# Activation tiles moved onto multiples of 256 bytes from the weight tiles, and one set of embedding weights split one channel group earlier

## The chip, the cores and the metric

The kernel runs on one core of a Trainium2 chip. TensorE (PE in the profile; PEld is its loading of the stationary operand) multiplies from SBUF into PSUM, ScalarE (ACT) and VectorE (DVE) work on SBUF and PSUM, GpSimd (POOL) does a few small things, and SyncE (SP) issues the DMAs. The metric is the device time of one execution in microseconds; the kernel before took 1401.75 (median of 3 runs, 1401.49 to 1403.82).

## The reference

A trunk of four layers over 256 tokens of width 1024, in float32. Each layer adds to the residual stream h a mixer of its normalised input (latent attention in layers 0 and 3, a Conformer convolution in layer 1, a gated recurrence in layer 2), then a SwiGLU feed-forward of width 2816, then a per-layer embedding gated by h:

```
for i in range(DEPTH):
    h = h + mixer(_rmsnorm(h, norm1_g[i]))
    h = h + _swiglu(_rmsnorm(h, norm2_g[i]), ffn_w_gu[i], ffn_w_down[i])
    gate = sigmoid(_rmsnorm(h, ple_norm_g[i]) @ ple_w_gate[i])
    h = h + (p[i] @ ple_w_proj[i]) * gate
```

The convolution of layer 1 is a gated pointwise product (2048 columns, one half through a sigmoid), a causal depthwise filter of 31 taps over each of 1024 channels, a layer norm over the channels, a swish and a second pointwise product (w_pw2).

## The kernel before

**Products.** A float32 weight tile arrives by DMA in a tile `raw`, and is split into two tiles in the matmul's rounded float32 format: ACT writes the high part `whi` (L189, or L194 where a norm's gain is multiplied in), DVE writes the rest `wlo` = raw - whi (L190 or L195). Activations are split in the same way after a transpose on TensorE (L259, L246, L247): `xT` for a whole normalised stream, `aT` for the gated inner values of the feed-forward, `cT` for attention's compressed vectors, `pT` for the embedding input. A product is three matmuls, high x high, low weights x high, high weights x low (`mm`, all recorded on L216). In most products the activation is stationary and 512 columns of weights move; in the convolution and in half of the recurrence the weights are stationary and 256 columns of xT move. In the profile's names `mm<-whi,xT` the tile behind the arrow is the one that moves, then the stationary one; `mm` and `acc` are PSUM banks.

**Where tiles lie.** Pools take SBUF one behind the other: constants, weights (`wpool`: 9 whi, 8 wlo, 4 raw tiles of 4096 bytes per partition), then `act` with everything that lives through the layers, then one pool per stage. Within a pool a tile stands behind those that were first asked for. Some of the tiles of `act` are scalars per token of 4 or 8 bytes, each of which takes 32; they stand between the large ones. The program's addresses, modulo 256:

| tiles | before | after |
|---|---|---|
| whi, wlo, raw, h | 224 | 224 |
| xT | 96 | 224 |
| pT, pph | 96 | 224 |
| th, hg, gain | 160 | 224 |
| aT, cT, and the stages' other first tiles | 160 | 224 |
| ident (constant) | 128 | 128 |

**The order of work.** Python issues the program; a scheduler places each instruction on its engine's queue, and each queue runs in that order. `self.fence` holds instructions behind which the next split of weights is to be issued (`behind`, around the splits in `granule` and `embed_weights`). In the convolution TensorE is pinned to the order in which the code is written.

**The convolution stage** (layer 1). For each of eight groups of 128 channels, c = 0 to 7, TensorE forms the pointwise product into a bank; ACT takes the sigmoid (L832) and DVE the gated value `glu` (L836): these two are `gate`. For c from 2 on the filter runs on TensorE: four DMAs per group make a shifted copy `win` (L763), one loads the taps as small matrices `tapw` (L767), 64 small matmuls sum them (`taps_pe`), and DVE (L782) or ACT turns the sum into `co`, of which ACT takes the square `sq` (L787). `moments` adds co and sq of two groups to the statistics on TensorE (`tr<-co,mean`, `tr<-sq,mean`). When all are in, `sums` is copied (L869), transposed by `tok`, copied (`st`, L874), and a chain of small DVE instructions gives scale and shift (dg, L884), which TensorE broadcasts (L885, `tr<-work,ones`). From there z, its swish and its split `yT` follow per group, and the product with w_pw2 (`linear_rows`, one weight granule per 128 rows). `embed_weights(2)` loads and splits p_t and two granules of ple_w_proj of the next layer; `embed(2)` multiplies them while the scale is worked out. Rows 0 to 4 of w_pw2 are split before the statistics, rows 5 to 7 during the swish.

Of the kernel before, what the change touches and what calls it, by code (L numbers as in the profile page):

```python
# [12 lines left out]
F32 = mybir.dt.float32  # L13
# [8 lines left out]
P = 128  # L22
# [29 lines left out]
GAINS = {}  # L52
for _k in GSIZE:
    GAINS[_k] = sum(GSIZE[j] * GCOUNT[j] for j in GAINS)


class Norm:
# [3 lines left out]
    def __init__(self, T, full=False, defer=False):  # L61
        self.T, self.full, self.defer = T, full, defer
        self.x, self.r = None, [None] * NT
# [64 lines left out]
class Trunk:  # L128
    def __init__(self, ctx, tc, a, out):
        self.ctx, self.tc, self.nc, self.a, self.out = ctx, tc, tc.nc, a, out  # L130
        nc = self.nc
        pool = lambda name, **k: ctx.enter_context(tc.tile_pool(name=name, **k))
        self.const = pool("const", bufs=1)
        self.wpool = pool("wpool", bufs=1)
        self.act = pool("act", bufs=1)
        self.ps = pool("ps", bufs=1, space=PSUM)
        self.n = 0
        self.fence = []
        self.head = None
        self.pinned = False  # L140
        self.pT, self.pph = {}, {}
        self.ident = self.const.tile([P, P], F32, name="ident")
        make_identity(nc, self.ident)
        self.gT = self.const.tile([P, a["gains"].shape[1]], F32, name="gT")
        self.h = [self.act.tile([P, D], F32, name=f"h{t}", tag=f"h{t}") for t in range(NT)]

    def nm(self, s):
# [8 lines left out]
        return self.bank("acc", 4)  # L156

    def tmp(self, tag, shape, bufs, dtype=F32, pool=None):
        return (pool or self.act).tile(shape, dtype, name=self.nm(tag), tag=tag, bufs=bufs)

    def scope(self, name):
        return self.tc.tile_pool(name=name, bufs=1)
# [404 lines left out]
    def mla(self, i, norm, done, pre):  # L567
# [8 lines left out]
        with self.scope(self.nm("mla")) as pool:  # L576
# [5 lines left out]
            for t in range(NT):  # L582
                xs, r = self.cut(norm.x, t), norm.r[t]
                pa, pb = self.acc(), self.acc()
                self.mms(pa[:, :QL], xs, [(hi[:, 0, :QL], lo[:, 0, :QL]) for hi, lo in gr])
                self.mms(pb[:, : KVL + ROPE], xs, [(hi[:, 0, QL : NC + ROPE], lo[:, 0, QL : NC + ROPE]) for hi, lo in gr])
                cg = tmp("cg", [P, NC], 1)
                nc.scalar.activation(cg[:, :QL], pa[:, :QL], AF.Copy)
                V.tensor_copy(cg[:, QL:], pb[:, :KVL])
                ss = tmp("css", [P, 2], 2)  # L590
                for c, (ps, n) in enumerate([(pa, QL), (pb, KVL)]):
                    nc.scalar.activation(self.tmp("junk", [P, 512], 1, BF16)[:, :n], ps[:, :n], AF.Square, scale=r, accum_out=ss[:, c : c + 1])
                kr = tmp("kr", [P, 1, ROPE], 2)
                nc.scalar.activation(kr[:, 0], pb[:, KVL : KVL + ROPE], AF.Copy, scale=r)
                self.split_T(cg, cT, 0, t)
                css.append(ss)
                krot.append(kr)
# [137 lines left out]
    def conv(self, i, norm, done, pre):  # L735
# [6 lines left out]
        PAD = TAPS - 1  # L742
# [3 lines left out]
        with self.scope(self.nm("conv")) as pool:  # L746
# [10 lines left out]
            def spread(c):  # L757

                win[c] = tmp("win", [P, QUAD, WIN], 3)
                for j in range(QUAD):  # L760
                    src = xin[c][32 * j : 32 * j + 32]
                    shifts = bass.AP(tensor=src.tensor, offset=src.offset, ap=[src.ap[0], [1, QUAD], [1, WIN]])
                    nc.sync.dma_start(win[c][:, j], shifts)  # L763

            def tap_weights(c):
                tapw[c] = tmp("tapw", [P, QUAD, STEPS, 32], 3)
                nc.sync.dma_start(tapw[c], a["conv_taps"][:, c])  # L767

            def taps_pe(c):
                ps = self.bank("mm", 2)[:, :S]  # L770
                for m in range(STEPS):
                    for j in range(QUAD):
                        self.matmul(
                            ps[32 * j : 32 * j + 32], tapw[c][:, j, m], win[c][:, j, QUAD * m : QUAD * m + S],
                            start=m == 0, stop=m == STEPS - 1,
                        )
                if c + 3 < KD:
                    tap_weights(c + 3)
                if c in BASE:
                    nc.scalar.activation(co[:, c], ps, AF.Identity, bias=par(c, TAPS))  # L780
                else:
                    V.scalar_tensor_tensor(out=co[:, c], in0=ps, scalar=par(c, TAPS), in1=self.base, op0=ALU.add, op1=ALU.subtract)  # L782
                    square(c)

            def square(c):
                sq[c] = tmp("sq", [P, S], 4)
                self.sq = nc.scalar.activation(sq[c], co[:, c], AF.Square)  # L787
# [15 lines left out]
            def chain(c, k0, k1):  # L803
                for k in range(k0, k1):
                    if k == 0:
                        V.tensor_scalar(out=co[:, c], in0=xin[c][:, :S], scalar1=par(c, 0), scalar2=par(c, TAPS), op0=ALU.mult, op1=ALU.add)
                    else:
                        V.scalar_tensor_tensor(out=co[:, c], in0=xin[c][:, k : k + S], scalar=par(c, k), in1=co[:, c], op0=ALU.mult, op1=ALU.add)

            def set_base():  # L810

                pm = self.bank("tr", 2)[:, :S]
                for b in BASE:
                    self.matmul(pm, self.mean, co[:, b], start=b == BASE[0], stop=b == BASE[-1])
                self.base = tmp("base", [P, S], 1)
                V.tensor_scalar(out=self.base, in0=pm, scalar1=KD / len(BASE), scalar2=None, op0=ALU.mult)
                for c in BASE:
                    V.tensor_tensor(out=co[:, c], in0=co[:, c], in1=self.base, op=ALU.subtract)
                    square(c)
# [4 lines left out]
            for c in range(KD):  # L824
                if c % 2 == 0:
                    ws = self.conv_head(i, c) if c else self.head
                ps = self.acc()
                for half in range(2):
                    s = slice(half * 256 + c % 2 * P, half * 256 + (c % 2 + 1) * P)
                    self.mms(ps[:, half * S : (half + 1) * S], [(hi[:, s], lo[:, s]) for hi, lo in ws], xs)  # L830
                sg = tmp("work", [P, S], 3)
                gate = [nc.scalar.activation(sg, ps[:, S:], AF.Sigmoid, bias=self.cb1[:, KD + c : KD + c + 1]).ins]  # L832
                x = xin[c] = tmp("glu", [P, PAD + S + 2], 4)
                nc.gpsimd.memset(x[:, :PAD], 0.0)
                nc.gpsimd.memset(x[:, PAD + S :], 0.0)
                glu = V.scalar_tensor_tensor(out=x[:, PAD : PAD + S], in0=ps[:, :S], scalar=self.cb1[:, c : c + 1], in1=sg, op0=ALU.add, op1=ALU.mult)  # L836
                gate.append(glu.ins)
                if c not in CHAINS:
                    spread(c)
                if c == 4:  # L840
                    taps_pe(2)
                if c == 5:
                    taps_pe(3)
                if c == 6:
                    set_base()
                    taps_pe(4)
                if c >= 2:
                    k = min(TAPS, 6 * (c - 1))
                    for b in CHAINS:
                        chain(b, 6 * (c - 2), k)  # L850
            taps_pe(5)
            moments(BASE)
            self.fence = gate
            self.embed_weights(2)
            rows = lambda k: self.granule([(a["conv_w_pw2"][0][k * P : (k + 1) * P], 0)], 1, D)
            ws = [rows(k) for k in range(5)]
            taps_pe(6)
# [319 lines left out]
```

## Time and profile before

| | |
|---|---|
| median of 3 runs | 1401.75 us |
| the profiled execution | 1402.8 us |
| its span, first to last instruction | 1401.0 us |
| mean granted TensorE clock | 0.992 |
| PE, DVE, ACT busy | 1352.4, 919.4, 789.7 us |

Matmuls are pipelined: the mean of one (about 400 ns for 512 columns) includes the way through the array and overlaps with the next, so the rate is read from start to start, or from pieces of the chain of waits, which give the time and the number of matmuls. That chain is followed back from the last instruction, at each step to what released it.

### The profile page before, as it was taken

Reading aid. Unit: us, or ns where it says so; the run is one execution under the profiler, and the core shown is the slowest. Engines: PE = TensorE matmul, PEld = TensorE weight load, DVE = VectorE, ACT = ScalarE, POOL = GpSimd, SP = SyncE. Lnnn points to the kernel's source line nnn. Section 1 sums busy time; section 2 is a strip of 40 time slices with the busy share of each in tenths; the row PEclk is TensorE's granted clock in tenths of the full one; section 3 lists DMA queues with packets and bytes.
Section 4 is the critical chain, followed back from the end, with each engine's and each line's share of the span. In section 5 each row is a group of like instructions: output and inputs, shape, how many; then the busy total and the mean of one; then the engine's idle time right before and its main releaser. Section 6 shows DMA issues by size and latency. Waiting matters only on the chain.

```text
span 1401.0 us, 20409 instructions
## 1 busy us (share of the span) xinstructions
PE 1352.4 (97%) x7153; PEld 1096.6 (78%) x7153; DVE 919.4 (66%) x1995; ACT 789.7 (56%) x1494; POOL 19.1 (1%) x52
## 2 busy tenths in 40 slices
PE   7899999999898999999999999999999999999997
PEld 6767878887875788887788887878878767888885
DVE  6867555558876855556887768555567776655556
ACT  6776555546525654555675546555556776555543
POOL 0100000000000000000000000000000000000000
PEclk9999999999998999999999999999999999999999
DMA  7524656536564655554474425555553433665532
GB/s 234 176 67 128 201 175 191 188 123 220 182 181 153 196 181 180 181 180 163 122 211 132 133 91 175 185 181 181 180 169 110 139 121 108 217 189 187 188 119 74
DMA packets 174023, 228.15 MB, mean 163 GB/s; under 512 B 11712, under 2 KB 138848, under 8 KB 173920
## 3 DMA queue, kind: packets, MB, share of 16 engines
q1 hardware_dynamic: 173920, 226.85, 51.6%
q8 instruction: 56, 0.92, 0.3%
q14 instruction: 47, 0.39, 0.1%
HBM read 222.27 MB, written 1.05 MB: 159 GB/s over the span
## 4 chain that ended last, share of the span: by engine, by line
PE 77%; DVE 8%; DMA 6%; ACT 6%; issue 2%; SPq 0%; DVEq 0%; ACTq 0%
PE mm L216 42%; PE acc L216 26%; PE tr L259 3%; DVE wlo L195 3%; ACT whi L194 2%; DMA raw<-in_ple_w_gate_dram 1%; PE acc L1020 1%; DMA raw<-in_conv_w_pw_dram 1%; DMA raw<-in_mla_w_in_dram 1%; DMA raw<-in_ffn_w_down_dram 1%; PE acc L659 1%; ACT p L669 1%; PE tr L641 1%; DVE wlo L190 1%; ACT whi L189 1%
## 5 line engine op out<-in xcount | busy, mean ns | idle before, releaser
L216 PE MATMUL mm<-whi,xT 128*128 128x512 f32 x1632 | 553.4, 402 | 1.0 <-ACT xT L246 0.7
L194 ACT ACTIVATE whi<-raw,gT 128x512 fp32r<-128x512 f32 (+3 forms) x604 | 387.7, 700 | 136.4 <-PE acc L216 60.1
L195 DVE SCALAR_TENSOR_TENSOR wlo<-raw,gT,whi 128x512 fp32r<-128x512 f32 (+3 forms) x604 | 410.4, 729 | 60.3 <-PE acc L216 33.9
L216 PEld LDWEIGHTS mm<-whi,xT 128*128 128x128 f32 x1632 | 306.3, 189 | 67.1 <-ACT xT L246 1.2
L216 PE MATMUL mm<-wlo,xT 128*128 128x512 f32 x816 | 323.7, 397 | 1.1 <-DVE wlo L190 1.1
L216 PE MATMUL acc<-whi,aT 128*128 128x512 f32 x704 | 234.5, 394 | 1.6 <-DVE aT L247 1.6
L190 DVE TENSOR_TENSOR wlo<-raw,whi 128x1024 fp32r<-128x1024 f32 x120 | 146.4, 1223 | 73.1 <-ACT whi L189 72.7
L189 ACT ACTIVATE whi<-raw 128x1024 fp32r<-128x1024 f32 x120 | 126.1, 1059 | 97.7 <-DMA raw<-in_ffn_w_down_dram 65.9
L216 PEld LDWEIGHTS mm<-wlo,xT 128*128 128x128 f32 x816 | 154.3, 189 | 32.1 <-DVE wlo L190 1.4
L216 PE MATMUL acc<-whi,xT 128*128 128x512 f32 (+2 forms) x544 | 168.9, 386 | 2.3 <-ACT xT L246 2.1
L216 PEld LDWEIGHTS acc<-whi,aT 128*128 128x128 f32 x704 | 131.7, 188 | 34.4 <-DVE aT L247 4.0
L216 PE MATMUL acc<-wlo,aT 128*128 128x512 f32 x352 | 137.6, 391 | 0.0
L373 DVE SCALAR_TENSOR_TENSOR ga<-mm,rs_y,sg 128x256 f32<-128x256 f32 x88 | 42.3, 481 | 142.3 <-ACT sg L371 142.3
L371 ACT ACTIVATE sg<-mm,rs_y 128x256 f32<-128x256 f32 x88 | 41.0, 466 | 138.7 <-PE mm L216 138.2
L216 PEld LDWEIGHTS acc<-whi,xT 128*128 128x128 f32 x544 | 100.5, 191 | 20.4 <-ACT xT L246 2.9
L216 PE MATMUL acc<-wlo,xT 128*128 128x512 f32 (+2 forms) x272 | 103.0, 381 | 0.0
L216 PEld LDWEIGHTS acc<-wlo,aT 128*128 128x128 f32 x352 | 66.1, 188 | 14.8
L247 DVE TENSOR_TENSOR aT<-tr,aT 128x256 fp32r<-128x256 f32 x88 | 37.0, 421 | 57.7 <-ACT aT L246 57.7
L216 PEld LDWEIGHTS acc<-wlo,xT 128*128 128x128 f32 x272 | 51.7, 190 | 8.7 <-DVE wlo L195 0.2
L216 PE MATMUL mm<-whi,cT 128*128 128x384 f32 (+1 forms) x160 | 51.1, 377 | 4.9 <-ACT q L629 3.3
L82 ACT ACTIVATE junk<-h 128x512 bf16<-128x512 f32 x48 | 30.0, 625 | 40.1 <-DVE h L348 22.4
L246 ACT ACTIVATE aT<-tr 128x256 fp32r<-128x256 f32 x88 | 32.7, 371 | 29.6 <-PE tr L259 29.6
(252 smaller groups left out, 1459.8 us busy)
## 6 DMA issues: line engine op xcount, KB each, us to landing
raw<-in_ffn_w_gu_dram SPq DMA_DIRECT2D x352, 256.0 KB, 4.3
raw<-in_ffn_w_down_dram SPq DMA_DIRECT2D x88, 512.0 KB, 4.3
raw<-in_ple_w_gate_dram SPq DMA_DIRECT2D x32, 512.0 KB, 4.9
raw<-in_hgrn_w_in_dram SPq DMA_DIRECT2D x64, 256.0 KB, 3.7
raw<-in_mla_w_out_dram SPq DMA_DIRECT2D x16, 512.0 KB, 4.4
raw<-in_conv_w_pw_dram SPq DMA_DIRECT2D x32, 256.0 KB, 4.9
raw<-in_mla_w_in_dram SPq DMA_DIRECT2D x16, 336.0 KB, 4.3
raw<-in_mla_w_uq_dram SPq DMA_DIRECT2D x12, 384.0 KB, 3.7
```

Of the source, the lines that this page charges most:

```text
L82: square = nc.scalar.activation(T.tmp("junk", [P, 512], 1, BF16), h[:, s], AF.Square, accum_out=ss[:, c : c + 1])
L189: self.last_split = nc.scalar.activation(hi[:, :used], raw[:, :used], AF.Copy)
L190: nc.vector.tensor_tensor(out=lo[:, :used], in0=raw[:, :used], in1=hi[:, :used].bitcast(F32), op=ALU.subtract)
L194: self.last_split = nc.scalar.activation(hi[:, s], raw[:, s], AF.Copy, scale=g[k])
L195: nc.vector.scalar_tensor_tensor(out=lo[:, s], in0=raw[:, s], scalar=g[k], in1=hi[:, s].bitcast(F32), op0=ALU.mult, op1=ALU.subtract)
L216: ins = self.nc.tensor.matmul(*args, **kw)
L246: a = self.nc.scalar.activation(hi, src, AF.Copy)
L247: v = self.nc.vector.tensor_tensor(out=lo, in0=src, in1=hi.bitcast(F32), op=ALU.subtract)
L259: nc.tensor.transpose(pt[:, (i - k0) * P : (i - k0 + 1) * P], src[:, i * P : (i + 1) * P], self.ident)
L371: nc.scalar.activation(sg, ps[:, :256], AF.Silu, scale=r)
L373: nc.vector.scalar_tensor_tensor(out=ga, in0=ps[:, 256:], scalar=r, in1=sg, op0=ALU.mult, op1=ALU.mult)
L641: nc.tensor.transpose(pt[:HD, h * P : (h + 1) * P], src[:, h], self.ident)
```

## The change

Two edits. The small tiles named in `SMALL` go to a pool of their own behind `act`, so that the large tiles of `act` follow each other without gaps; a tile of 16 floats that nothing uses fills that pool, so that the stages' pools begin at 224 modulo 256 as well (table above). And `embed_weights(2)` is called behind the gating of the seventh channel group (c = 6) and no longer behind that of the eighth.

```diff
--- before.py
+++ after.py
@@ -52,6 +52,11 @@
 GAINS = {}
 for _k in GSIZE:
     GAINS[_k] = sum(GSIZE[j] * GCOUNT[j] for j in GAINS)
+
+
+
+SMALL = ("ss", "sst", "rs_m", "rs_y", "rs_h", "rs_t", "rhalf")
+PAD = 16
 
 
 class Norm:
@@ -133,6 +138,7 @@
         self.const = pool("const", bufs=1)
         self.wpool = pool("wpool", bufs=1)
         self.act = pool("act", bufs=1)
+        self.small = pool("small", bufs=1)
         self.ps = pool("ps", bufs=1, space=PSUM)
         self.n = 0
         self.fence = []
@@ -142,6 +148,7 @@
         self.ident = self.const.tile([P, P], F32, name="ident")
         make_identity(nc, self.ident)
         self.gT = self.const.tile([P, a["gains"].shape[1]], F32, name="gT")
+        self.small.tile([P, PAD], F32, name="pad", tag="pad")
         self.h = [self.act.tile([P, D], F32, name=f"h{t}", tag=f"h{t}") for t in range(NT)]
 
     def nm(self, s):
@@ -156,7 +163,7 @@
         return self.bank("acc", 4)
 
     def tmp(self, tag, shape, bufs, dtype=F32, pool=None):
-        return (pool or self.act).tile(shape, dtype, name=self.nm(tag), tag=tag, bufs=bufs)
+        return (pool or (self.small if tag in SMALL else self.act)).tile(shape, dtype, name=self.nm(tag), tag=tag, bufs=bufs)
 
     def scope(self, name):
         return self.tc.tile_pool(name=name, bufs=1)
@@ -844,6 +851,9 @@
                 if c == 6:
                     set_base()
                     taps_pe(4)
+                    self.fence = gate
+                    self.embed_weights(2)
+                    self.fence = []
                 if c >= 2:
                     k = min(TAPS, 6 * (c - 1))
                     for b in CHAINS:
@@ -851,7 +861,6 @@
             taps_pe(5)
             moments(BASE)
             self.fence = gate
-            self.embed_weights(2)
             rows = lambda k: self.granule([(a["conv_w_pw2"][0][k * P : (k + 1) * P], 0)], 1, D)
             ws = [rows(k) for k in range(5)]
             taps_pe(6)
```

The line numbers of the changed kernel are 7 higher from `tmp` on, and 9 higher behind the moved call. Instructions on TensorE and GpSimd keep their order. On ACT, ahead of the changed place the sigmoid of c = 6 stands; before, the three squares and the sigmoid of c = 7 (L832) come next, then pT, two proj granules and row 0 of w_pw2:

```order
L787 ACTIVATE sq_4225<-co_3574 128x256
L787 ACTIVATE sq_4228<-co_3574 128x256
L787 ACTIVATE sq_4266<-co_3574 128x256
L832 ACTIVATE work_4329<-acc_4280,cb_1800 128x256
L246 ACTIVATE pT_4383<-raw_4385 128x512
L189 ACTIVATE whi_4389<-raw_4391 128x1024
L189 ACTIVATE whi_4395<-raw_4397 128x1024
L189 ACTIVATE whi_4401<-raw_4403 128x1024
L787 ACTIVATE sq_4376<-co_3574 128x256
L189 ACTIVATE whi_4407<-raw_4409 128x1024
L189 ACTIVATE whi_4413<-raw_4415 128x1024
L787 ACTIVATE sq_4465<-co_3574 128x256
```

With the change (L253 and L196 are the splits, L794 the squares, L839 the sigmoid of c = 7):

```order
L253 ACTIVATE pT_4272<-raw_4274 128x512
L196 ACTIVATE whi_4278<-raw_4280 128x1024
L196 ACTIVATE whi_4284<-raw_4286 128x1024
L794 ACTIVATE sq_4229<-co_3578 128x256
L794 ACTIVATE sq_4232<-co_3578 128x256
L794 ACTIVATE sq_4270<-co_3578 128x256
L839 ACTIVATE work_4351<-acc_4302,cb_1804 128x256
L196 ACTIVATE whi_4405<-raw_4407 128x1024
L196 ACTIVATE whi_4411<-raw_4413 128x1024
L196 ACTIVATE whi_4417<-raw_4419 128x1024
L196 ACTIVATE whi_4423<-raw_4425 128x1024
L794 ACTIVATE sq_4398<-co_3578 128x256
```

pT and the two proj granules moved ahead of the squares; rows 0 to 3 of w_pw2 now stand together behind the sigmoid of c = 7, ahead of the square of c = 5. On DVE, from the glu of c = 7 on, before:

```order
L836 SCALAR_TENSOR_TENSOR glu_4331<-acc_4280,cb_1800,work_4329 128x256
L247 TENSOR_TENSOR pT_4384<-raw_4385,pT_4383 128x512
L190 TENSOR_TENSOR wlo_4390<-raw_4391,whi_4389 128x1024
L190 TENSOR_TENSOR wlo_4396<-raw_4397,whi_4395 128x1024
L782 SCALAR_TENSOR_TENSOR co_3574<-mm_4342,cpar,base_4222 128x256
L190 TENSOR_TENSOR wlo_4402<-raw_4403,whi_4401 128x1024
L190 TENSOR_TENSOR wlo_4408<-raw_4409,whi_4407 128x1024
L782 SCALAR_TENSOR_TENSOR co_3574<-mm_4431,cpar,base_4222 128x256
L190 TENSOR_TENSOR wlo_4414<-raw_4415,whi_4413 128x1024
L190 TENSOR_TENSOR wlo_4420<-raw_4421,whi_4419 128x1024
L190 TENSOR_TENSOR wlo_4426<-raw_4427,whi_4425 128x1024
L782 SCALAR_TENSOR_TENSOR co_3574<-mm_4477,cpar,base_4222 128x256
```

and with the change, from the same glu (L843; L197 writes wlo, L789 co) to the co of c = 7:

```order
L843 SCALAR_TENSOR_TENSOR glu_4353<-acc_4302,cb_1804,work_4351 128x256
L197 TENSOR_TENSOR wlo_4406<-raw_4407,whi_4405 128x1024
L197 TENSOR_TENSOR wlo_4412<-raw_4413,whi_4411 128x1024
L197 TENSOR_TENSOR wlo_4418<-raw_4419,whi_4417 128x1024
L789 SCALAR_TENSOR_TENSOR co_3578<-mm_4364,cpar,base_4226 128x256
L197 TENSOR_TENSOR wlo_4424<-raw_4425,whi_4423 128x1024
L197 TENSOR_TENSOR wlo_4430<-raw_4431,whi_4429 128x1024
L789 SCALAR_TENSOR_TENSOR co_3578<-mm_4435,cpar,base_4226 128x256
L789 SCALAR_TENSOR_TENSOR co_3578<-mm_4481,cpar,base_4226 128x256
```

pT and the first two wlo are gone from here (they stand ahead of the co of c = 4), and the co of c = 6 and c = 7 now follow each other behind the fifth row's wlo. On SP, from row 0 of w_pw2 on, before (the four-fold rows are the windows of c = 6 and c = 7):

```order
L185 DMA raw_4403<-in_conv_w_pw_dram 128x1024
L767 DMA tapw_4108<-in_conv_taps_dram 128x1024
L763 DMA win_4214<-glu_4210 128x1x284 x4
L767 DMA tapw_4263<-in_conv_taps_dram 128x1024
L763 DMA win_4335<-glu_4331 128x1x284 x4
L185 DMA raw_4409<-in_conv_w_pw_dram 128x1024
L185 DMA raw_4415<-in_conv_w_pw_dram 128x1024
L185 DMA raw_4421<-in_conv_w_pw_dram 128x1024
L185 DMA raw_4427<-in_conv_w_pw_dram 128x1024
L185 DMA raw_4620<-in_conv_w_pw_dram 128x1024
```

and with the change (L192 weights, L774 taps, L770 windows):

```order
L192 DMA raw_4407<-in_conv_w_pw_dram 128x1024
L774 DMA tapw_4112<-in_conv_taps_dram 128x1024
L770 DMA win_4218<-glu_4214 128x1x284 x4
L192 DMA raw_4413<-in_conv_w_pw_dram 128x1024
L192 DMA raw_4419<-in_conv_w_pw_dram 128x1024
L774 DMA tapw_4267<-in_conv_taps_dram 128x1024
L192 DMA raw_4425<-in_conv_w_pw_dram 128x1024
L770 DMA win_4357<-glu_4353 128x1x284 x4
L192 DMA raw_4431<-in_conv_w_pw_dram 128x1024
L192 DMA raw_4624<-in_conv_w_pw_dram 128x1024
```

Rows 1, 2 and 3 of w_pw2 moved ahead of the windows of c = 7, rows 1 and 2 ahead of the last taps too; the loads of p_t and ple_w_proj, further up, did not move.

## The prediction

> **What bounds the kernel now.** I read the page's shares first, then the chain of waits for where the work is regular, then a timeline of the one stage that the moved call touches.
>
> ```profile
> PE 1352.4 (97%) x7153; PEld 1096.6 (78%) x7153; DVE 919.4 (66%) x1995; ACT 789.7 (56%) x1494; POOL 19.1 (1%) x52
> PE 77%; DVE 8%; DMA 6%; ACT 6%; issue 2%; SPq 0%; DVEq 0%; ACTq 0%
> L216 PE MATMUL mm<-whi,xT 128*128 128x512 f32 x1632 | 553.4, 402 | 1.0 <-ACT xT L246 0.7
> L216 PE MATMUL mm<-wlo,xT 128*128 128x512 f32 x816 | 323.7, 397 | 1.1 <-DVE wlo L190 1.1
> L216 PE MATMUL acc<-whi,xT 128*128 128x512 f32 (+2 forms) x544 | 168.9, 386 | 2.3 <-ACT xT L246 2.1
> L216 PE MATMUL acc<-whi,aT 128*128 128x512 f32 x704 | 234.5, 394 | 1.6 <-DVE aT L247 1.6
> L216 PE MATMUL mm<-whi,cT 128*128 128x384 f32 (+1 forms) x160 | 51.1, 377 | 4.9 <-ACT q L629 3.3
> L216 PE MATMUL acc<-xT,whi 128*128 128x256 f32 x256 | 47.7, 288 | 0.6 <-DVE xT L247 0.3 <-ACT xT L246 0.2
> ```
>
> TensorE carries 77% of the chain that ends last, and almost nothing stands before its matmuls: in the feed-forward stages, most of the program, time falls only if a matmul gets shorter. The busy means (402 ns) overlap; what counts is the distance from start to start, which the chain of waits shows, first in a gate of layer 0 (xT stationary, into acc), then in the feed-forward stage of layer 1 (mm: xT, acc: aT):
>
> ```profile
> 325.40 4.90 PE acc L216 x21
> 546.15 4.18 PE mm L216 x18
> 550.34 2.76 PE acc L216 x12
> 588.95 4.20 PE mm L216 x18
> ```
>
> Both kinds multiply 512 columns of the same weight tiles (224 bytes past a multiple of 256). With xT as the stationary operand (96 past) one takes 4.18/18 = 232.2 ns, with aT (160 past) 2.76/12 = 230.0. The operands are 128 bytes out of step in the first and 64 in the second: and the bank is not the cause, since xT into acc takes 4.90/21 = 233. I put the step at 2.3 ns. Where the granted clock fell to half, three matmuls took 439.43 - 438.15 = 1.28 us:
>
> ```profile
> 433.50:436.00 2.50, 2.50 (x9) 2.00 (x8) 0.42 (x1) 0.68 (x2) 0.00 (x0) 0.50 0.73 233
> 438.15 1.05 PE L216 MATMUL mm<-whi,pT 128*128 128x512 f32 x2
> 439.43 1.05 PE L216 MATMUL mm<-whi,pT 128*128 128x512 f32 x2
> 553.16 0.40 PE L216 MATMUL mm<-wlo,xT 128*128 128x512 f32 x1
> 553.17 0.42 PEld L216 LDWEIGHTS mm<-whi,xT 128*128 128x128 f32 x2
> ```
>
> That is 427 ns each, exactly twice 213, so at full clock xT's loses 19 ns and aT's nearly 17 to something that vanishes when the array reads at half its rate. And the load of the next stationary operand starts 0.01 us after each matmul (last two rows), so two streams read SBUF side by side, each from its own starting offset. An influence of offsets is thus plausible, and small so far.
>
> **The address part.** It adds no work. xT goes from 96 to 224, pT likewise, aT and cT from 160 to 224: every pair of weights and activations becomes 0 bytes out of step (mod 256), a distance that no fp32r pair in this trace has. Count of the pairs, by the rows above, wlo's always half of whi's as in the first two: xT stationary 1632 + 816 + 544 + 272 = 3264; xT moving, 256 columns, 256 + 128 into acc and as many into mm = 768; pT 96; so 4128 leave a distance of 128. aT 704 + 352, cT 160 + 80: 1296 leave a distance of 64. What a distance of 0 costs is unknown; bounds come from the two distances seen. I take the value of 64 for it: the cost fell from 128 to 64, so 0 continues in that direction, and fp32 transposes, which read two streams as well, show no penalty at any distance:
>
> ```profile
> L259 PE MATMUL tr<-ident,ga 128*128 128x128 f32 x176 | 33.8, 273 | 1.5 <-DVE ga L373 1.3 <-DVE rs_y L287 0.2
> L688 PE MATMUL tr<-ident,p 128*128 128x128 f32 x32 | 8.4, 273 | 0.0
> L348 DVE TENSOR_TENSOR h<-acc,h 128x512 f32<-128x512 f32 x26 | 17.8, 688 | 8.1 <-PE acc L216 8.1
> L461 DVE TENSOR_TENSOR h<-h,th 128x512 f32<-128x512 f32 x16 | 11.0, 689 | 0.2
> ```
>
> (ident stands at 128, ga at 160, p at 128: 273 ns both.) VectorE does not care: 688 ns with one SBUF operand, 689 with two that are 64 apart. So 4128 x 2.3 ns = 9.5 us, of which I count the part that lies on the chain. The chain holds 42% (mm) and 26% (acc) of L216, 953 us; all these matmuls, start to start, are about 4560 x 0.23 less 40 for the narrower ones, plus 768 x 0.12, some 1100 to 1150. So 0.83, and **7.9 us**. Ends: one more step down would give 4.6 ns on the 4128 and 2.3 on the 1296, 18.2 us; two steps up from xT's cost 23.2 us.
>
> **The moved call.** Today the embedding weights (p_t, two proj granules) are split behind the gating of the last channel group, with raw tiles landed 20 us earlier; four raw tiles exist, and these three hold them.
>
> ```profile
> 394.66 1.67 SPq L185 DMA_DIRECT2D raw<-in_ple_w_proj_dram  x2
> 400.62 0.55 SPq L185 DMA_DIRECT2D raw<-in_conv_w_pw_dram  x1
> 404.51 0.47 ACT L832 ACTIVATE work<-acc,cb 128x256 f32<-128x256 f32 x1 [5.38 <-PE acc L216]
> 415.30 0.62 ACT L246 ACTIVATE pT<-raw 128x512 fp32r<-128x512 f32 x1
> 415.82 2.94 ACT L189 ACTIVATE whi<-raw 128x1024 fp32r<-128x1024 f32 x3
> 405.62 2.98 SPq L763 DMA_DIRECT2D win<-glu  x4
> 416.04 2.96 SPq L763 DMA_DIRECT2D win<-glu  x4
> 419.09 11.28 SPq L185 DMA_DIRECT2D raw<-in_conv_w_pw_dram  x7
> 422.55 3.64 PE L216 MATMUL mm<-win,tapw 128*32 128x256 f32 x64
> 423.66 1.06 ACT L189 ACTIVATE whi<-raw 128x1024 fp32r<-128x1024 f32 x1 [3.55 <-DMA raw<-in_conv_w_pw_dram]
> 427.87 0.40 PE L216 MATMUL tr<-sq,mean 128*32 128x256 f32 x1 [1.27 <-ACT sq L787]
> 429.12 0.40 PE L216 MATMUL tr<-sq,mean 128*32 128x256 f32 x1 [0.63 <-ACT sq L787]
> 429.51 1.06 ACT L189 ACTIVATE whi<-raw 128x1024 fp32r<-128x1024 f32 x1 [0.45 <-DMA raw<-in_conv_w_pw_dram]
> 430.60 1.23 DVE L190 TENSOR_TENSOR wlo<-raw,whi 128x1024 fp32r<-128x1024 f32 x1 [0.58 <-ACT whi L189]
> 431.75 0.48 DVE L782 SCALAR_TENSOR_TENSOR co<-mm,cpar,base 128x256 f32<-128x256 f32 x1
> 432.28 1.06 PE L216 MATMUL tr<-co,mean 128*32 128x256 f32 x2 [2.53 <-DVE co L782]
> 436.05 0.16 DVE L874 COPY st<-tr 128x4 f32<-128x4 f32 x1 [1.80 <-PE tr L216]
> 439.09 0.28 DVE L884 TENSOR_SCALAR work<-ident,rs_y 128x128 f32<-128x128 f32 x1
> 441.32 1.25 PE L885 MATMUL tr<-work,ones 128*128 128x128 f32 x8
> ```
>
> Rows 1 to 4 of the second pointwise weights are issued only from 419.09, behind the last windows. Row 4 is split on ACT at 429.51 and on DVE at 430.60, and the last channel's statistics input (co, 431.75) stands behind it on DVE; TensorE waits until 432.28.
>
> Now the three splits come behind the seventh group's sigmoid (404.51 + 0.47). On ACT they end near 405.0 + 0.6 + 2 x 1.06 = 407.7, on DVE, with three lo parts and two base subtractions, near 410. Both engines were idle there (5.4 us before the next group's sigmoid on ACT). Queued behind them are three squares and a co that TensorE wants from 418 on. On SP the embedding loads stay where they are; rows 1 to 3 move ahead of the last windows, two of them ahead of the last taps too. SP, past the seventh group's windows at 408.6, issues rows 1 and 2, the last taps, and row 3 near 410: 2 MB that land by about 417, in time for the taps (422.55) as well. Behind the last sigmoid ACT splits rows 0 to 3 from 415.4 without waiting, to 419.6; DVE gets to channel 5's co at about 420.1 and its square is done at 421.0, before TensorE asks, ahead of the last taps at 422.55. Row 4 alone still stands behind the last windows, issued at 419.1, and lands some 4.5 us later, as row 1 does today (419.09 to 423.66): split on ACT by 424.5, on DVE by 425.8. Then channel 6's co and square (426.6), and channel 7's, whose taps end near 426.1 as today: last statistics near 426.7 instead of 432.28: **5.6 us**. If row 4 is 2 us slower, 3.6.
>
> The gaps (1.3, 0.6 and 2.5 us) that vanish also led the clock to half: windows of the granted clock read 0.50 from 433.5 on. From the first row at 432.28 to the copy st at 436.05 is 3.77 us, of which nearly all is TensorE at half rate (2.1 at full); from there TensorE arrives at the broadcast (ones) 5.27 us later at 441.32, where at full rate DVE's work tile is the limit, 3.3 us (439.37). So 1.65 + 1.95 = **3.6 us** more, if the clock holds; I think it does, since one gap of 0.6 us is left. The following matmuls over yT wait on this chain alone, so the gain goes through. Lower end of this part: 3.6 (row late, clock falls anyway), upper 9.2, which I take.
>
> **Sum.** The profiled execution took 1402.8 (span 1401.0 and 1.8 around it), 1.05 above the median. 1402.8 - 7.9 - 9.2 = 1385.7, and by the median's distance 1384.6: **1385 us**.
>
> **The rivals.**
> - *Addresses do nothing* (the 2.3 ns between xT and aT has another cause, such as how the two chains are broken up by transposes). For it: the step is 1%. Against it: xT is as slow in either bank. Then 1401.75 - 9.2 = 1392.5.
>   The Trainium skill ("SBUF — State Buffer", Who interferes with whom) says that TensorE's moving operand and its weight load have independent read ports and that TensorE never waits on anyone; by that rule this rival holds. The 427/2 against 232 above speaks against its letter, but not for any particular distance.
> - *Only 128 matters.* If the banks repeat every 128 bytes, xT is already in step and slow, aT out of step and fast; then xT keeps its time and aT and cT lose 2.3 ns: 1296 x 2.3 x 0.83 = +2.5, with the call 1395.0.
> - *In step is best by a further step*: -18.2 - 9.2, 1374.3.
>   By the Trainium skill ("TensorE: Matmul & The Clock Gate", Wait — 56ns, not 53.3ns?) warm matmuls of 512 columns follow each other at 215.7 ns; were all of the rest of xT's 232 due to addresses, the gain would be an estimated 70 us. No run here shows so short a step.
> - *In step is worst, slower than before.* Load and matmul start 0.01 us apart; read from the same offset they could meet at the same bank at once and at every line. Priced at two steps up, 4128 x 4.6 and 1296 x 6.9 ns, times 0.83: +23.2 - 9.2 = +14, 1415.8. It decides as soon as the average matmul loses over 9.2/(0.83 x 5424) = 2.0 ns. Against it: the trend from 128 to 64, and the transposes.
>
> **How the numbers follow.** Forecast 0.46, nothing 0.13, only 128 0.12, further step 0.14, worst 0.15. All but the last end below 1396; the conv part's lower end brings half of "only 128" and some of "nothing" to within 0.2% (2.8 us), which is about what a measurement of this kernel can tell from no change. So faster 0.77, same 0.08, slower 0.15. The range leaves out the worst case and the tail of the further step: 1370 to 1400; the forecast's own is 1380 to 1391.
>
> **What would show it.** Right: in feed-forward stages "mm L216 x18" near 4.14 us and "acc L216 x12" still 2.75; granted clock 1.00 from 426 to 440; no idle over 1 us before the last statistics; the last statistics some 8 us earlier in the span (2 to 3 from addresses, 5.6 from the call). Wrong: x18 unchanged (addresses do nothing, or 128 decides, if x12 grows to 2.79), or above 4.25 (worst). If TensorE still stops for a DMA of conv_w_pw before the statistics, the call's part is wrong.

## The result and the profile after

The changed kernel took 1386.24 us (median of 4 runs, 1384.47 to 1389.05) against 1401.86 for the kernel before: a ratio of 0.989, 95% interval 0.9874 to 0.9906, faster by 15.6 us. Four later runs, beside an experiment, gave 1384.40 (ratio 0.9872, 0.9854 to 0.9891). The forecast was 1385. The profiled execution took 1385.44 (span 1383.7). The page's shares and groups:

```profile
PE 1334.1 (96%) x7153; PEld 1091.4 (79%) x7153; DVE 918.5 (66%) x1995; ACT 788.2 (57%) x1494; POOL 17.6 (1%) x52
PE 76%; DVE 9%; DMA 6%; ACT 6%; issue 3%; SPq 0%; DVEq 0%; ACTq 0%
L223 PE MATMUL mm<-whi,xT 128*128 128x512 f32 x1632 | 547.4, 398 | 1.0 <-ACT xT L253 0.7
L223 PE MATMUL acc<-whi,aT 128*128 128x512 f32 x704 | 232.2, 391 | 1.5 <-DVE aT L254 1.4
L223 PE MATMUL acc<-xT,whi 128*128 128x256 f32 x256 | 48.2, 290 | 0.4 <-ACT xT L253 0.2
```

TensorE is busy 18.3 us less and bounds the kernel as before. The chain of waits gives the rate, here layer 1's feed-forward stage and, first, the convolution's products with xT moving (239 matmuls of 256 columns):

```profile
353.58 30.11 PE acc L223 x239
602.88 4.13 PE mm L223 x18
607.00 2.72 PE acc L223 x12
611.31 4.10 PE mm L223 x18
```

The first row's counterpart in the kernel before:

```profile
355.54 29.98 PE acc L216 x239
```

Eighteen matmuls over xT take 4.09 to 4.14 us where they took 4.17 to 4.20, and twelve over aT 2.72 where they took 2.75 or 2.76. So aT gained too, though the forecast had it unchanged; the convolution's narrow products lost a little, 30.11 us for 29.98. Taken from all starts that follow each other without a wait:

```
columns, stationary operand     before     after
512, xT                          232.5      228.3 ns
512, aT                          229.7      227.1
384, cT                          173.4      174.6
384, xT                          176.0      174.9
256, whi (xT moves)              118.6      119.7
```

By these, 3072 x -4.2, 1056 x -2.6 and 768 x +1.1 make -14.8 us; the differences of all single steps that changed by no more than 20 ns add up to -14.1.

The convolution, in rows of the timeline (ACT, DVE, SP, TensorE by time):

```profile
403.70 1.99 ACT L196 ACTIVATE whi<-raw 128x1024 fp32r<-128x1024 f32 x2
405.37 2.35 DVE L197 TENSOR_TENSOR wlo<-raw,whi 128x1024 fp32r<-128x1024 f32 x2
408.97 0.38 SPq L192 DMA_DIRECT2D raw<-in_conv_w_pw_dram  x1
413.64 2.94 ACT L196 ACTIVATE whi<-raw 128x1024 fp32r<-128x1024 f32 x3
417.00 1.06 ACT L196 ACTIVATE whi<-raw 128x1024 fp32r<-128x1024 f32 x1 [0.42 <-DMA raw<-in_conv_w_pw_dram]
417.88 2.21 SPq L192 DMA_DIRECT2D raw<-in_conv_w_pw_dram  x4
421.83 1.06 ACT L196 ACTIVATE whi<-raw 128x1024 fp32r<-128x1024 f32 x1 [2.77 <-DMA raw<-in_conv_w_pw_dram]
422.92 1.23 DVE L197 TENSOR_TENSOR wlo<-raw,whi 128x1024 fp32r<-128x1024 f32 x1 [3.18 <-ACT whi L196]
424.06 1.02 DVE L789 SCALAR_TENSOR_TENSOR co<-mm,cpar,base 128x256 f32<-128x256 f32 x2
424.57 1.34 ACT L794 ACTIVATE sq<-co 128x256 f32<-128x256 f32 x4 [1.69 <-DVE co L789]
425.35 0.40 PE L223 MATMUL tr<-sq,mean 128*32 128x256 f32 x1 [0.41 <-ACT sq L794]
426.03 0.38 PE L223 MATMUL tr<-co,mean 128*32 128x256 f32 x1
427.98 0.16 DVE L883 COPY st<-tr 128x4 f32<-128x4 f32 x1 [0.81 <-PE tr L223]
431.45 1.32 PE L894 MATMUL tr<-work,ones 128*128 128x128 f32 x8 [0.21 <-DVE work L893]
```

The embedding weights are split by 407.7, rows 0 to 3 of w_pw2 follow from 413.64 with one wait of 0.42 us, and only row 4 comes late, from a load issued at 417.88. Its split on DVE still stands ahead of the last two co, their squares wait for these, and TensorE for the first square. TensorE waits 0.41 us ahead of the last statistics where it had waited 1.27, 0.63 and 2.53. The granted clock stays up, as a row of the windows shows (its last three numbers are the clock, the DMA share and GB/s):

```profile
428.50:431.00 2.50, 2.50 (x13) 1.92 (x11) 2.08 (x15) 1.20 (x2) 0.00 (x0) 1.00 0.00 0
```

TensorE's instructions stand in the same order in all kernels of this study, so the start of each can be set against the same one's elsewhere. At the taps of c = 6 and 7 the changed kernel is 1.7 us ahead of the kernel before, at the last statistics 6.3, at the first product over yT 9.8, at the end 17.4. So 8.1 us of the gain arise between the taps of c = 6 (417 us) and the product over yT (435 us), and 9.2 elsewhere. (The split yT is written to a tile that the profile calls xT.)

### The profile page after: what moved, and what is told of

The parts are those of the page before. It is cut to its first block, busy times and chain, and to the rows that moved or that the text cites. A ratio compares the mean times of both kernels' runs of the same rounds, so it can differ in the third digit from the quotient of the medians.

```text
span 1383.7 us, 20410 instructions
## 1 busy us (share of the span) xinstructions
PE 1334.1 (96%) x7153; PEld 1091.4 (79%) x7153; DVE 918.5 (66%) x1995; ACT 788.2 (57%) x1494; POOL 17.6 (1%) x52
## 4 chain that ended last, share of the span: by engine, by line
PE 76%; DVE 9%; DMA 6%; ACT 6%; issue 3%; SPq 0%; DVEq 0%; ACTq 0%
PE mm L223 40%; PE acc L223 26%; DVE wlo L202 3%; PE tr L266 3%; DMA raw<-in_ffn_w_down_dram 2%; DMA raw<-in_ple_w_gate_dram 1%; ACT whi L201 1%; PE acc L1029 1%; DMA raw<-in_mla_w_in_dram 1%; ACT whi L196 1%; DVE wlo L197 1%; PE acc L666 1%; ACT p L676 1%; DMA raw<-in_conv_w_pw_dram 1%; DMA raw<-in_mla_w_ukv_dram 1%
## 5 line engine op out<-in xcount | busy, mean ns | idle before, releaser
L223 PE MATMUL mm<-whi,xT 128*128 128x512 f32 x1632 | 547.4, 398 | 1.0 <-ACT xT L253 0.7
L197 DVE TENSOR_TENSOR wlo<-raw,whi 128x1024 fp32r<-128x1024 f32 x120 | 146.3, 1224 | 70.8 <-ACT whi L196 68.8
L196 ACT ACTIVATE whi<-raw 128x1024 fp32r<-128x1024 f32 x120 | 126.1, 1059 | 95.7 <-DMA raw<-in_ffn_w_down_dram 52.7
L223 PEld LDWEIGHTS acc<-wlo,aT 128*128 128x128 f32 x352 | 66.1, 188 | 13.5
L223 PE MATMUL acc<-xT,whi 128*128 128x256 f32 x256 | 48.2, 290 | 0.4 <-ACT xT L253 0.2
```

The source lines that it names most:

```text
L196: self.last_split = nc.scalar.activation(hi[:, :used], raw[:, :used], AF.Copy)
L197: nc.vector.tensor_tensor(out=lo[:, :used], in0=raw[:, :used], in1=hi[:, :used].bitcast(F32), op=ALU.subtract)
L223: ins = self.nc.tensor.matmul(*args, **kw)
```

## The experiments

**One part at a time.** Addresses without the moved call:

```diff
-                    self.fence = gate
-                    self.embed_weights(2)
-                    self.fence = []
...
             self.fence = gate
+            self.embed_weights(2)
             rows = lambda k: ...
```

> The changed kernel with the embedding weights' call back behind the last group's gating: only the addresses differ from the kernel before. Theory (the two parts add up): read off the traces, address gains are -9.2 us of the -17.4 and the call -8.2, so about 1392.6 us, with 4.11 us for 18 matmuls over xT and 2.72 for 12 over aT as in the changed kernel, the gaps of 1.3, 0.6 and 2.5 us in the convolution back, and the granted clock at 0.50 behind them. Rival (the call does nothing by itself, faster operands bring the splits into step): 1386 to 1388 us and no drop of the clock.

Measured: 1391.06 us (5 runs), 11.3 below the kernel before, ratio 0.9925 (0.9913 to 0.9937). The chain in the feed-forward stage and, behind "...", timeline and clock windows of the convolution:

```profile
578.47 4.11 PE mm L223 x18
582.58 2.72 PE acc L223 x12
...
431.05 1.06 PE L223 MATMUL tr<-co,mean 128*32 128x256 f32 x2 [1.97 <-DVE co L789]
433.50:436.00 2.50, 2.50 (x9) 2.17 (x8) 1.03 (x7) 0.00 (x0) 0.00 (x0) 0.50 0.34 119
```

The gaps (0.68, 1.13 and 1.97 us here) and the clock at 0.50 are back, although the operands are faster: the rival falls.

The moved call alone, on the kernel before:

```diff
                     set_base()
                     taps_pe(4)
+                    self.fence = gate
+                    self.embed_weights(2)
+                    self.fence = []
...
             self.fence = gate
-            self.embed_weights(2)
             rows = lambda k: ...
```

> The kernel before with only the call moved behind the seventh group's gating; all addresses as before. Theory (the parts add up): -8.2 us, about 1393.6 us; 4.18 and 2.76 us in the feed-forward stage as before; last statistics 4.6 us earlier than before and the granted clock 1.00 from 426 to 440 us. Rival (the clock falls anyway, it is a matter of load and not of the gaps): -4.6 us, 1397.2. Rival (hidden anyway): 1401.5.

Measured: 1395.32 us (6 runs), 7.1 below the kernel before, ratio 0.9960 (0.9944 to 0.9975). Chain, then a window of the convolution:

```profile
598.75 4.18 PE mm L216 x18
602.93 2.76 PE acc L216 x12
...
431.00:433.50 2.50, 2.50 (x13) 1.93 (x11) 2.08 (x15) 1.19 (x2) 0.00 (x0) 1.00 0.00 0
```

The rates are the old ones and the clock is up, so both rivals (the clock falls anyway, the gain is hidden anyway) fall. From the taps of c = 6 to yT this kernel takes as long as the changed one, to 0.1 us: 8.2 us less than before, in that place alone. The two ratios multiplied give 0.9885, and the changed kernel's are 0.9890 and 0.9872: the parts add up, within the intervals.

**The distance by itself.** Behind the end of the changed kernel, groups of 36 matmuls over two tiles, with nothing else at work (m and s are the byte offsets of the moving and the stationary operand):

```diff
+            mov = self.tmp("bmov", [P, 1152], 1, F32R, pool)
+            sta = self.tmp("bsta", [P, 1152], 1, F32R, pool)
...
+            for m, s, cols, rows, same in BENCH:
+                for g in range(4):
+                    ps = self.acc()
+                    for k in range(9):
+                        o = s // 4 + (0 if same else k % 6 * 128)
+                        self.matmul(ps[:rows, :cols], sta[:, o : o + rows], mov[:, m // 4 : m // 4 + cols], start=k == 0, stop=k == 8)
```

> The changed kernel with 42 groups of 36 extra matmuls behind its end, on two tiles of their own, with no other engine at work on them: the stationary operand d bytes past the moving one (mod 256), for 512, 384, 256 and 128 columns, then both shifted together, then 64 stationary columns, then one stationary operand repeated; its time is longer by the extra matmuls (some 280 us). Theory (distance alone sets it): 512 columns: d = 0 227 ns, 64 and 192 230, 128 232.5, steps of 4 to 16 between 227 and 229; 256 columns: 120 at 0, 118.6 at 128; 384: 174.7 at 0, 173.4 at 192, 176 at 128; shifted together at d = 0: 227 everywhere. Rival (not the distance but where the tile lies in a line of 256): shifted together gives other values, up to 232. Rival (traffic of the other engines is needed): all near 227.

Measured, mean ns from start to start (the whole run, 1652.48 us, is longer by these matmuls):

```
512 columns, stationary d bytes past the moving operand
 d     0     4     8    16    32    64    96   112   128   160   192   224   256
   226.7 232.5 230.5 233.3 233.4 233.2 234.3 233.4 233.5 233.4 229.2 233.4 226.7
 d          0    32    64    96   128   160   192   224
256 col 119.8 118.3 117.8 117.3 118.7 119.7 117.8 117.8
384 col 173.5     -  176.7     - 176.0     - 173.3     -
128 col 110.1     -  111.6     - 111.6     - 111.6     -
d = 0, both shifted by 32: 228.6 (one step of 286 in it); by 64, 96, 128, 160: 227.4 each
64 stationary columns: 230.2 (d = 0), 229.3 (d = 128)
one stationary operand repeated: 226.7 (d = 0), 232.4 (d = 128)
```

No other engine is needed, and the place in a line of 256 bytes does not count, only the distance (tried at distance 0). That much of the theory stood. But the distance has no slope and no symmetry: 192 is good and 64 is not, and 32 is as slow as 128. At 256 columns in step is the slowest, with 160. In the kernel the products over aT take what they take alone (227.1 ns), but those over xT 228.3, 1.6 more; what adds that was not tried.

> The changed kernel with 90 groups of 18 extra matmuls behind its end, on two tiles of their own: 512 columns with the stationary operand 0, 8, 16 ... 504 bytes past the moving one, and six distances between; then 128 to 480 columns in step, and 128 to 448 at a distance of 160. Theory (in step, mod 256, is one point and not the end of a slope): 226.7 at 0 and 256, about 229 at 192 and 448, 230 to 234 everywhere else; in step each matmul loses the same 13 ns at all lengths from 256 on (320 columns 147 ns, 448 200 ns). Rival (a slope towards 0): values fall steadily from 128 down to 0 and up to 256, with 8 and 248 near 227.

Measured, the same groups at finer steps (18 matmuls each, 1720.11 us in all). Two rows of the timeline, the first for d = 0 alone, the second for d = 128 with one matmul of the group ahead:

```profile
1377.11 4.25 PE L229 MATMUL acc<-bmov,bsta 128*128 128x512 f32 x18
1443.71 4.59 PE L229 MATMUL acc<-bmov,bsta 128*128 128x512 f32 x19
```

From their starts: 226.7 at 0, 226.9 at 120, 228.2 at 240, 228.9 at 192, 230 to 231 at 8, 24, 152, 176, 200 and 232, and 231.8 to 234.3 elsewhere; from 256 on every value comes again (376: 226.9), to 0.2 ns except at 256 itself (227.9, after 226.7 in the first series). Neighbours of a good distance are bad (112: 233.3, 128: 232.8, 248: 233.2). So it repeats every 256 bytes and is good at isolated points among those tried; the rival's slope is refuted. In step, 256, 320, 384 and 512 columns take 13.2, 13.0, 13.5 and 13.3 ns more than half of the 427 ns of a matmul at the half clock, scaled by the columns, but 288 columns take 11.8, 416 14.9, 448 16.6 and 480 17.1 more: my "same 13 ns at all lengths" does not hold there.

**In the kernel.** xT 64 bytes past the weights, aT at 32, 96, 128 and 160 in layers 0 to 3:

```diff
-        self.small.tile([P, PAD], F32, name="pad", tag="pad")
+        self.small.tile([P, 64], F32, name="pad", tag="pad")
...
+        self.act.tile([P, 16], F32, name="xpad", tag="xpad")
...
         with self.scope(self.nm("ffn")) as pool:
+            pool.tile([P, (8, 24, 32, 40)[i]], F32, name=self.nm("apad"), tag="apad")
```

> The changed kernel with xT and pT 64 bytes past the weights (mod 256) and aT at another distance in each layer's feed-forward stage: 32, 96, 128 and 160 in layers 0 to 3. Theory (distance alone, and the same from both sides): 18 matmuls over xT 4.14 us, 12 over aT 2.74 in layer 0, 2.78 in layer 1, 2.79 in layer 2, 2.78 in layer 3. Rival (the step between xT and aT comes from the chain they stand in, not from their distance): 4.11 and 2.72 in all layers.

Measured: 1398.52 us (1 run). Layer 1 in the chain:

```profile
574.84 4.20 PE mm L224 x18
579.03 2.80 PE acc L224 x12
```

4.20 and 2.80 stand there in all four layers: 233.3 ns at 64, 32, 96, 128 and 160 alike, as in the matmuls measured alone (and 2.80 is slower than aT's 2.76 at 192). The size of my theory's steps was wrong; that distance decides was right, and the rival (the chain they stand in) falls. 13.1 us of the gain are lost against the changed kernel's profiled execution, with the convolution's gain kept.

**Loads or splits?** Rows 1 to 4 are loaded behind the last windows, as before, with the embedding weights split early (`hold` is the last window's DMA; while it is set, a load of weights is issued behind it):

```diff
+                if c == KD - 1:
+                    self.hold = ins.ins
...
-            ws = [rows(k) for k in range(5)]
+            hold, self.hold = self.hold, None
+            ws = [rows(0)]
+            self.hold = hold
+            ws += [rows(k) for k in range(1, 5)]
+            self.hold = None
```

> The changed kernel with the loads of rows 1 to 4 of the second pointwise weights held behind the last group's windows on SP, where they were before; the embedding weights are still split behind the seventh group. Theory (the lateness of before came from the loads, which the raw tiles held up): the last statistics fall back to about 430 us, the clock falls too, and the product over yT starts some 7 us later than in the changed kernel, 1393 us. Rival (it came from the three splits that stood in ACT's and DVE's queues): within 1 us of the changed kernel, 1386 to 1387.

Measured: 1386.97 us (1 run). ACT, TensorE and a clock window:

```profile
420.81 1.06 ACT L200 ACTIVATE whi<-raw 128x1024 fp32r<-128x1024 f32 x1 [4.01 <-DMA raw<-in_conv_w_pw_dram]
428.37 1.06 PE L227 MATMUL tr<-co,mean 128*32 128x256 f32 x2 [2.15 <-DVE co L795]
428.50:431.00 2.50, 2.50 (x7) 1.23 (x7) 0.42 (x1) 1.75 (x3) 0.00 (x0) 0.50 0.85 288
```

The wait of 2.15 us and the half clock return. Counted from the taps of c = 6, the last statistics come 3.3 us later than in the changed kernel, of 4.6 in the kernel before, and yT's product 5.7 of 8.1. So late loads alone account for some 70% of the part. The rest is what the splits in the queues would explain; late splits with early loads were not tried. That it is the moved call which lets the loads go is shown by the call alone: rows 1 and 2 are issued from 409.61 us there, row 1 only at 419.09 in the kernel before. The total does not show the 5.7 us: at the end this run is only 1.5 us behind, having been 1 us ahead by 420 us already and having made up more in later stages, in waits that differ by a us or two from run to run. One run's total cannot tell the two; the place in the trace can.

**Gap and clock.** Three copies on VectorE ahead of the last co (eight in the second kernel), all else as in the changed kernel:

```diff
+                    if c == KD - 1:
+                        for _ in range(3):
+                            V.tensor_copy(self.tmp("hg", [P, D], 1)[:, :S], ps)
                     V.scalar_tensor_tensor(out=co[:, c], in0=ps, ...)
```

> The changed kernel with three copies of the last taps' sum on VectorE ahead of the last channel's co (some 3 x 0.45 = 1.35 us): TensorE waits that much longer before the last statistics, all loads and splits as in the changed kernel. Theory (gaps in TensorE's work lead the granted clock down): a gap of about 1.8 us in place of 0.41; yT's product starts 1.4 us later than in the changed kernel if so short a gap is borne, up to 4.9 if the clock falls. Rival (the clock fell for another cause, such as the late loads): +1.4 and the clock at 1.00.

> The same with eight copies (8 x 0.45 = 3.6 us): one gap of about 4 us ahead of the last statistics, nothing else as in the kernel before. Theory (gaps lead the clock down): 0.50 for some 10 us behind the gap, and yT's product starts 3.6 + 3.5 = 7 us later than in the changed kernel. Rival (another cause): the clock at 1.00, 3.6 us later.

Measured with three: 1384.40 us (1 run); the clock stays at 1.00 and yT's product comes 0.8 us later (counted as above). But TensorE waited 0.30 us only, the rest of the copies lay beside other statistics, so this kernel says little. With eight, 1390.93 us (1 run), TensorE and a clock window:

```profile
427.93 0.40 PE L223 MATMUL tr<-sq,mean 128*32 128x256 f32 x1 [1.31 <-ACT sq L797]
431.11 0.62 PE L223 MATMUL tr<-co,mean 128*32 128x256 f32 x2 [2.12 <-DVE co L792]
433.50:436.00 2.50, 2.50 (x8) 2.02 (x8) 1.85 (x13) 0.29 (x1) 0.00 (x0) 0.50 0.00 0
```

Gaps of 1.31 and 2.12 us bring the clock to 0.50 with early splits and, but for row 4, early loads. The last statistics come 3.4 us later and yT's product 5.3: the half clock costs 1.9 us here, not 3.5, and lasts some 7 us, not 10. The theory holds, its size was too large. The low stretch lasts 10.24 us in the kernel before and with the addresses alone, 6.83 here and with the held loads, and 3.41 at 352.9 us in the changed kernel: in these traces it comes in steps of 3.41 us, so its cost is not in proportion to the gap.

How large a gap is borne, the changed kernel's second profiled execution (further down) shows better than the three copies. TensorE waits 1.07 us there ahead of the same statistics, and the granted clock stays at 1.00:

```profile
426.82 0.40 PE L223 MATMUL tr<-sq,mean 128*32 128x256 f32 x1 [1.07 <-ACT sq L794]
```

With the held loads, waits of 0.35, 0.63 and 2.15 us within 4.4 us were enough for 0.50.

**The gain given back.** Four more raw tiles in the feed-forward stage's own pool, for half of its granules:

```diff
-        raw = self.tmp("raw", [P, 1024], 4, pool=self.wpool)
+        self.turn += 1
+        if self.extra is not None and self.turn % 8 < 4:
+            raw = self.tmp("rawx", [P, 1024], 4, pool=self.extra)
+        else:
+            raw = self.tmp("raw", [P, 1024], 4, pool=self.wpool)
...
             for j in range(NJ):
+                self.extra = pool if 0 < j < NJ - 1 else None
```

> The changed kernel with four more raw tiles, in the feed-forward stage's own pool (half of its weight granules from the second of eleven blocks on use them). Theory (the faster matmuls run into loads that come late because four raw tiles hold them up, as the waits for ga and, behind it on ACT, for ffn_w_down show): those waits, 4 us in the changed kernel's four feed-forward stages, go, 1382 to 1383 us. Rival (the loads are late by themselves, or whi and wlo hold them up): 1386, within 1 us of the changed kernel.

> The changed kernel once more, beside the one with more raw tiles and against the kernel before: 1386 us, ratio 0.989, if nothing but chance stood between its first four runs (1384.5 to 1389.1); for the sum of the two parts done alone (-11.3 and -7.1 us) it would have to be 1384.

Measured: 1382.31 us (4 runs, 1379.97 to 1383.13) beside 1384.40 for the changed kernel (4 runs, 1382.33 to 1386.45), ratios to the kernel before 0.986 (0.9842 to 0.9877) and 0.9872. Waits in layer 0's feed-forward stage (total, times, longest in us), first of the changed kernel:

```profile
PE tr L266 <- DVE ga L380: 2.3, 2, 1.7
ACT whi L196 <- DMA raw<-in_ffn_w_down_dram: 14.5, 10, 3.5
```

and of the kernel before:

```profile
PE tr L259 <- DVE ga L373: 0.9, 1, 0.9
ACT whi L189 <- DMA raw<-in_ffn_w_down_dram: 18.0, 16, 2.8
```

ACT waits for late loads in both. With the extra tiles the wait for ga is gone in all four layers; in layer 0 these are left on TensorE and for the same loads on ACT:

```profile
PE acc L228 <- DVE aT L259: 0.5, 1, 0.5
ACT whi L201 <- DMA raw<-in_ffn_w_down_dram: 1.6, 2, 0.9
```

Over the four layers ACT waits 52.7 us for ffn_w_down in the changed kernel's first trace, 52.6 in its second, and 5.4 with the extra tiles. So the loads were late because raw tiles held them up. What that lateness costs TensorE is less sure. Its waits for ga are 4.2 us in the changed kernel's first trace, 1.4 in its second and none with the held loads, where four raw tiles serve as before; they are 1.3 in the kernel before and none with the call alone. So they differ between runs by as much as the theory's 4 us, and that the faster matmuls bring them is not shown. The profiled span with extra tiles is 4.5 us shorter than the changed kernel's beside it, the median 2.1; the runs of the two overlap, so whether and how much it is faster stays open. Its median is the lowest of the kernels here. The changed kernel's own second median, 1384.40, is near what the parts done alone add up to (1384), and the median of its eight runs is 1385.0.

## Why the prediction was right, and where it was not

The time was right to about a us, and its two terms held as parts: addresses 11.3 us (7.9 forecast), the call 7.1 by medians and 8.1 by the trace (9.2). The first was too small and the second too large, and these errors partly cancel in the sum; the first also rests on a step that was wrong.

- *Operands' offsets matter; addresses do nothing* (rival). The first is shown by the addresses alone (0.9925) and by matmuls alone, 226.7 against 233.4 ns with no other engine at work. The Trainium skill's rule ("SBUF — State Buffer", Who interferes with whom), by which TensorE's two reads have independent ports and TensorE waits on nobody, does not hold as it stands: the two times differ. Where in the chip the time goes, no run shows.
- *"The cost fell from 128 to 64, so 0 continues in that direction."* This step failed. There is no slope: what I called 64 out of step is 192 as the stationary operand stands to the moving one, one of a few good points; at 64 it costs 233. Two distances can't show a law, and I read a direction into them. That 0 is good was luck as far as this argument goes. The transposes that were to show no penalty could not have told: matmuls of 128 columns alone take 110.1 to 111.6 ns at all four distances tried. "Only 128 matters" is refuted too: 128 is slow, 256 is 0 again.
- *2.3 ns on 4128 matmuls, 9.5 us.* Mis-sized: -4.2 on the 512-column products over xT, and -2.6 on the 1056 over aT, counted at nothing, while the 768 narrow ones, counted as a gain, lost 1.1. Together -14.1 to -14.8. Per matmul this is near the rival "a further step" (4.6 and 2.3), as the 2.72 us for twelve products over aT show, where the forecast had 2.75. That rival's time, 1374.3, is missed all the same: the narrow products lost, not all of the gain arrived (next point), and the call gave less than 9.2.
- *0.83 of it lies on the chain.* The matmuls alone (the single steps counted in the result) are 14.1 to 14.6 us shorter in all nine traces with the new addresses. Of 14.3 us in the addresses-only trace 10.1 arrived, of the changed kernel's 14.1 9.2; but 10.8 of 14.4 in its second trace and 13.4 of 14.3 with the held loads, each without the call's part. By medians it is 11.3 (8.8 to 12.2 by the interval) of 14.3, so 0.83 stands near the upper end and is not refuted. What the share is in one execution depends on TensorE's waits, which differ by a us or two in several stages from run to run; which of them answer to the addresses was not tried one by one.
- *"In step is worst", slower.* False for 512 columns; for the 256-column products it is nearly so, which are too few to decide.
- *The call, 5.6 us to the last statistics.* It was 4.6, and the term mis-sized is the stretch behind row 4. Row 4 was split when forecast: by 424.15 us on DVE, which is 425.8 with the 1.7 us added that this kernel was ahead by then. But from there to the last statistics I had allowed 0.9 us (425.8 to 426.7), for the last two co and squares; it took 1.9 (424.15 to 426.03). Row 4 is still the limit: with the call alone, in the changed kernel's second trace and with more raw tiles it is 1.9 us too, while the time from the last taps to the last statistics differs by 0.7. No gap over 1 us was left in the first trace, as forecast; in the second, where row 4's split ends at 425.62, one of 1.07 us was.
- *The clock, 3.6 us.* 427.98 - 426.03 = 1.95 us (2.1 forecast) and 431.45 - 427.98 = 3.47 (3.3 forecast): 3.6. That gaps are the cause is shown by the eight copies, which bring the half clock back; that late loads are enough for most of the gaps, by the held loads.
- The Trainium skill's 215.7 ns ("TensorE: Matmul & The Clock Gate", Wait — 56ns, not 53.3ns?) is reached at no distance: the best is 226.7, so the estimate of 70 us had no ground here.

## What to carry to other kernels

Where TensorE streams matmul after matmul, the distance between moving and stationary tiles, mod 256, is worth a measurement by itself before a model: a few groups behind the kernel's end show it in one run, and it depends on the number of columns. Two points never make a trend. A gain per instruction does not arrive whole: here about a fifth of it was missing by the medians, and the share differed from trace to trace. Waits ahead of a small serial stage can cost twice, since the clock falls behind them once they are long enough: here 3.1 us in all were, and 1.07 was not.

## What the runs showed of the hardware

- A 512-column matmul of rounded float32 with its load takes 226.7 to 226.9 ns at distances 0 and 120 (mod 256 bytes), 228 to 229 at 240 and 192, and 230 to 234 at the others tried; neighbours 8 bytes away are slow. The same distances rank otherwise at 256 columns (117.3 at 96, 119.8 at 0).
- Even the best distance leaves 13 ns over the 213.4 that half of the half-clock time (427 ns) gives.
- Gaps of 1.31 and 2.12 us within 4.5 us were enough for the granted clock to fall to 0.50 for some 7 us; single ones of 0.41 and 1.07 were not. The low stretches last 3.41, 6.83 or 10.24 us.
